# A hybrid decoder layer on one core: the low-rank products of decay and rate from stacked rounded parts

## The chip, the core and the metric

The kernel runs on one core of one Trainium2 chip. TensorE multiplies and transposes, VectorE (DVE in the profile), ScalarE (ACT) and GpSimd (POOL) do the element work, SyncE (SP) issues most of the DMAs, and each engine takes its own program in order, with semaphores between them. The metric is the device time of one launch, in microseconds. Before the change it is 3192.13 us, the median of three runs (3189.84 to 3195.04).

## The reference

One layer on a prompt of 2048 rows and, beside it, 8 sequences of 4 sample rows with stored state. A row has 1024 columns. The normalised rows go through one wide projection into a short gated convolution and an RWKV-7 recurrence of 16 heads of 64 columns. The two are merged by gates and projected back. Cut to the part around the change:

```python
h = _rmsnorm(x, norm_g)
p = jnp.einsum('bsd,dn->bsn', h, w_in)          # 10368 columns
...
xm = p_rwkv + (prev - p_rwkv) * mu_shift
r, k, v, wd, ad, zr = _split(xm, RWKV_SIZES)    # wd and ad: 64 columns each
w_logit = w0 + jnp.einsum('bsr,rc->bsc', jnp.tanh(wd), w_up)
w_log = (-jax.nn.softplus(-w_logit.astype(jnp.float32)) - 0.5)
decay = jnp.exp(-jnp.exp(w_log))
a = jax.nn.sigmoid((a0 + jnp.einsum('bsr,rc->bsc', ad, a_up)).astype(jnp.float32))
...
S = (S * d_t[:, :, None, :] + sa[..., None] * (kk_t * a_t)[:, :, None, :]
     + v_t[..., None] * k_t[:, :, None, :])
y = jnp.einsum('bhvk,bhk->bhv', S, r_t)
```

The two low-rank products are the `einsum` with `w_up` (the decay, from `tanh(wd)`) and the one with `a_up` (the rate, from `ad`). Each contracts over 64 columns and gives 1024.

## The kernel before

**Sets, pairs, blocks.** The prompt rows are taken in four sets (`th` 0 to 3) of `NT` = 512, transposed so that columns lie on the partitions; the last set has the 32 sample rows beside its 512 and the stored rows behind them. Per set the projection runs through blocks of 128 weight columns (`Block`). A block's weights (1024 x 128) are two rounded parts, `whl`: the high part is a copy into the F32R type, the low part what remains. In the first set both are made from `wraw` (ACT copies, DVE subtracts, L236 and L249) and stored in scratch; later sets load them back. `proj` (L266) issues 24 matmuls per block and 512 columns: for each eighth of the contraction high weights by high rows `XH`, low weights by `XH`, and high weights by `XL`, all into the bank `ip`. They are the bulk of TensorE's program. Weights are fetched up to `WAHEAD` = 4 blocks ahead.

**Side programs.** A set has 8 pairs of heads, 128 columns each, so 32 pairs in all. A pair's work beyond the projection stands in generators, each a `Side` (L309): `rwkv_keys` (norms, low-rank products, decay, scaled keys `AR` and `BK`), `rwkv_solve` (scores `GM` and the inversion of triangular blocks: `Mc`, its transposed form `Mi`, and 31 steps of `tt` and `X`), `rwkv_merge` (from `Xo` to the inverse `Xbd`, with the small products through `T11` and `Wm`), `rwkv_load` (`SV`, `BKt`), `rwkv_chain` (the state) and `rwkv_out`. `drive` (L351) walks the projection matmul by matmul and after each lets the sides go on; how far, a planner decides: each side has a weight (`SIDES`, L25) to be spent over a stretch of the main stream (`over`, `CUTS`), and goes on only when `Clock`, a model of the engines' times fed by each traced instruction (L111 to L153), says that its operands will be ready and its banks free. So what one instruction is thought to cost decides where later ones of all sides stand. The order on each engine is then fixed in the program. All instructions go through one helper, so the profile gives them L121; they are told apart by their tiles.

**The state chain.** `rwkv_chain` (L1091) takes a pair's eight chunks of 64 rows, each a step: `pa` (state `S` by `AR`), `us` (two DVE additions), `pb` from `us` and `Xbd`, `SV` (one half copied by DVE, then one by ACT), `pb` from `SV` and `BKt`, and the update of `S` (two on DVE, with `sp` from ACT). Each waits for the one ahead of it; on TensorE projections are laid between them. While pair k is in its chain, keys, solve, merge and load of pair k + 1 run on the same engines.

**The low-rank products.** `lora_block` (L763) is the set's first block of the recurrence: its 128 output columns are `wd` and `ad`. `alloc` forces the keys of the set before to their end (`need`), since those read the one tile `lora`; `end` takes the tanh of the upper 64 partitions. In `rwkv_keys` (L808) SP loads the pair's 64 x 128 of `w_up` and of `a_up` into the two halves of `up`; two plain fp32 matmuls, each over 64 partitions, fill two banks `pt`, and ACT takes a tanh of each (with the biases `w0h` and `a0h`). A +1 on ACT and a scan on DVE, with the mask `rst`, follow. An fp32 matmul shows as two passes in the trace, an F32R one as one.

Of the kernel before, what the change touches and what calls it, by code (L numbers as in the profile page):

```python
# [7 lines left out]
F32 = mybir.dt.float32  # L8
# [171 lines left out]
def hybrid_kernel(tc, x_prompt, x_sample, state_conv, state_shift, state_rwkv, norm_g, w_in, conv_w,  # L180
# [238 lines left out]
    SV = xp.tile([P, NC1, P], F32, name="SV")  # L419
    early = {}  # L420
# [69 lines left out]
    rst = con.tile([P, NT], F32, name="rst")  # L490
    V.memset(rst, 1.0)
    V.memset(rst.rearrange("p (c t) -> p c t", t=C)[:, :, 0:1], 0.0)
    rst_s = con.tile([P, NSAMP], F32, name="rst_s")
# [265 lines left out]

    cur = {}  # L760
    job = {}

    def lora_block(th):  # L763

        def alloc():
            need(job.get(("keys", th * NB - 1)))
            return rw.tile([P, NT + NSAMP], F32, name="lora")

        def end(t):
            nt = NTT[th]  # L770
            A.activation(out=t[0:64, 0:nt], in_=t[0:64, 0:nt], func=AF.Tanh)
            cur["lora"] = t
        return mixed_block(th, ("lora", th), WCOL[:, RW0 + 3 * D:RW0 + 3 * D + P], 3 * NB, alloc, end)

# [28 lines left out]
    HS = [slice(0, 64), slice(64, 128)]  # L803

# [3 lines left out]
    def rwkv_keys(th, p, o):  # L808
# [7 lines left out]
        up = sm.tile([P, P], F32, name="up")  # L816
        for k, src in enumerate((w_up, a_up)):
            SP.dma_start(out=up[HS[k]], in_=src[0][:, p * P:(p + 1) * P])

# [14 lines left out]
        yield W["norm"], [up], 2  # L834
# [4 lines left out]
        for (c0, c1) in sg:  # L839
            if c0:  # L840
                yield 0.0, (), 2
            pts = [new_pt([P, 512], F32, name="pt") for _ in range(2)]
            for k in range(2):
                T.matmul(pts[k][:, 0:c1 - c0], lhsT=up[HS[k]], rhs=lt[HS[k], c0:c1], start=True, stop=True)
            for k, (dst, bias) in enumerate(((L, w0h), (ta, a0h))):
                A.activation(out=dst[:, c0:c1], in_=pts[k][:, 0:c1 - c0], func=AF.Tanh, scale=0.5, bias=bias[:, p:p + 1])
# [134 lines left out]
    def rwkv_merge(th, p, o):  # L981
# [8 lines left out]
        T11 = rw.tile([P, NCH, 32], F32, name="T11")  # L990
# [3 lines left out]
        Wm = rw.tile([P, NCH, 32], F32, name="Wm")  # L994
# [404 lines left out]
    for t in (BK[:, NCH], ARB[0][:, NCH], ARB[1][:, NCH], *XB):  # L1399
        G.memset(t, 0.0)  # L1400
# [11 lines left out]
    def begin_pair(th, p, total):  # L1412
# [7 lines left out]
        job["keys", k] = Side(rwkv_keys(th, p, o), "keys", [prior("load", k - 1), prior("solve", k - 1)] + read(k - 2)).over(0, f[3])  # L1420
# [20 lines left out]
    for th, hv, p, nx in plan:  # L1441
        total = length(hv)
        if p is None:
            job["prep", 0, 1] = Side(prep(0, 1), "first").over(0, EDGE / 2 * NB)
            Side(zero_rest(), "zero").over(1.5 * NB, 2 * NB)
# [177 lines left out]
```

## Time and profile before

| | |
|---|---|
| time, median of 3 runs | 3192.13 us |
| the profiled execution | 3193.32 us, of which the span (first to last instruction) is 3191.6 |
| granted TensorE clock, mean | 0.992 |
| projections `ip<-XH,whl` and `ip<-XL,whl` | 7776 and 3888 matmuls, 2105.1 and 1364.0 us busy |
| low-rank products `pt<-lora,up` | 160 passes, 46.8 us busy |
| first matmul group of the low-rank products, last one | 63.0 us, 2506.6 us |
| TensorE busy from 25 to 760 us | 705.90 of 735 |
| TensorE busy from 760 to 1395 us | 624.22 of 635 |
| TensorE busy from 2900 us to the end | 278.30 of 291.6 |

Matmuls overlap their neighbours, so busy sums of groups exceed what the groups cost; the cost of a few matmuls is read from the starts of those around them. In rows of the time line the columns are the start, the duration, the engine, the line, the operation, output<-inputs, for matmuls the tile of the array, the shape, and how many like instructions in succession the row stands for; in brackets stands how long the engine had idled and for what. In rows of equal stretches the busy times of PE, PEld, DVE, ACT and POOL follow the length, then granted clock, DMA share and GB/s.

### The profile page before, as it was taken

The numbers are of one execution on the slowest core, as the hardware profiler recorded it, in microseconds if no ns is written. First come the engines' busy times: TensorE is split into PE (matmuls) and PEld (weight loads), VectorE is DVE, ScalarE is ACT, GpSimd is POOL, SyncE is SP. The second block draws the span as 40 slices with busy tenths as digits, with TensorE's granted clock in tenths as the row PEclk, the third lists the DMA queues.
The fourth block names the chain that finished last, engine by engine and source line by source line (L and its number), as shares of the span: only waits on it lengthen the run. The fifth ranks groups of instructions, "written<-read, shape, count | busy, mean of one in ns | idle before, by whom it ended". The sixth has DMA issues, their size and how long they took to land.

```text
span 3191.6 us, 55625 instructions
## 1 busy us (share of the span) xinstructions
PE 3092.0 (97%) x21530; PEld 2596.5 (81%) x21530; DVE 1992.5 (62%) x5704; ACT 1241.9 (39%) x2571; POOL 309.6 (10%) x517
## 2 busy tenths in 40 slices
PE   7999999999999999999999999999999999999998
PEld 6777777887777778877777789989889889778896
DVE  5687777776666666666666676766677664443332
ACT  5454445444333434434443334344444432211201
POOL 2011111111000001100101010000000000000000
PEclk9999999999999999999999999999999999999999
DMA  8786666644444444444444444434443469988863
GB/s 267 258 267 220 213 212 220 207 173 148 146 162 160 155 159 159 169 157 153 159 153 158 159 147 142 138 127 139 144 143 135 138 223 318 363 337 304 316 241 120
DMA packets 241504, 615.09 MB, mean 193 GB/s; under 512 B 33931, under 2 KB 143620, under 8 KB 187479
## 3 DMA queue, kind: packets, MB, share of 16 engines
q1 hardware_dynamic: 241094, 611.00, 55.8%
q8 instruction: 170, 2.79, 0.4%
q14 instruction: 96, 0.78, 0.1%
q0 software_dynamic: 144, 0.52, 0.0%
HBM read 452.10 MB, written 159.36 MB: 192 GB/s over the span
## 4 chain that ended last, share of the span: by engine, by line
PE 69%; DVE 18%; ACT 5%; issue 5%; DMA 3%; POOL 1%; SPq 0%; ACTq 0%; DVEq 0%; POOLq 0%
PE ip L121 49%; PE pt L121 10%; PE po L121 6%; PE pb L121 3%; DVE X L121 2%; DVE tmp L121 2%; DVE tt L121 2%; ACT tmp L121 2%; DVE Mi L121 2%; DVE whl L121 1%; DVE us L121 1%; PE pa L121 1%; DVE S L121 1%; DMA wraw<-in_w_in_dram 1%; ACT Xbd L121 1%
## 5 line engine op out<-in xcount | busy, mean ns | idle before, releaser
L121 PE MATMUL ip<-XH,whl 128*128 128x512 f32 (+3 forms) x7776 | 2105.1, 351 | 6.6 <-DVE gt L121 3.9
L121 PEld LDWEIGHTS ip<-XH,whl 128*128 128x128 f32 x7776 | 1342.0, 190 | 178.3 <-issue 27.5
L121 PE MATMUL ip<-XL,whl 128*128 128x512 f32 (+3 forms) x3888 | 1364.0, 351 | 2.7 <-POOL XL L121 2.6
L121 PEld LDWEIGHTS ip<-XL,whl 128*128 128x128 f32 x3888 | 738.5, 190 | 79.0 <-issue 7.0
L121 DVE TENSOR_TENSOR X<-X,tt 128x60 f32<-128x60 f32 (+24 forms) x992 | 211.7, 213 | 27.5
L121 DVE TENSOR_TENSOR tt<-Mi,X 128x60 f32<-128x60 f32 (+24 forms) x992 | 209.9, 212 | 27.4
L121 DVE SCALAR_TENSOR_TENSOR S<-pb,pe,sp 64x64 f32<-64x64 f32 x512 | 143.8, 281 | 106.6 <-PE pb L121 100.5
L121 ACT ACTIVATE sp<-S,pe 128x128 f32<-128x128 f32 x256 | 99.5, 400 | 244.7 <-DVE S L121 241.2
L121 ACT ACTIVATE tmp<-ip,vec 128x512 f32<-128x512 f32 (+2 forms) x174 | 103.2, 593 | 231.6 <-PE ip L121 230.2
L121 ACT COPY SV<-pb 64x64 f32<-64x64 f32 x256 | 53.3, 208 | 329.2 <-DVE SV L121 325.5
L121 DVE TENSOR_TENSOR whl<-wraw,whl 128x1024 fp32r<-128x1024 f32 x105 | 134.2, 1279 | 58.0 <-ACT whl L121 57.7
L121 PE MATMUL po<-whl,MH 128*128 128x512 f32 x544 | 170.4, 394 | 0.0
L121 DVE TENSOR_TENSOR us<-pa,P 64x64 f32<-64x64 f32 x512 | 110.2, 215 | 45.2 <-PE pa L121 33.7
L121 PEld LDWEIGHTS pb<-us,Xbd 128*128 128x128 f32 x512 | 85.9, 189 | 56.9 <-PE ip L121 21.5
L121 PE MATMUL ip<-RH,whl 128*128 128x512 f32 (+2 forms) x512 | 128.4, 341 | 1.7 <-DMA whl<-w_or 1.6
L121 PEld LDWEIGHTS pb<-SV,BKt 128*128 128x128 f32 x512 | 85.1, 189 | 54.6 <-ACT SV L121 45.9
L121 ACT CAST whl<-wraw 128x1024 fp32r<-128x1024 f32 x105 | 109.5, 1044 | 50.5 <-DMA wraw<-in_w_out_r_dram 14.8
L121 PE MATMUL pb<-SV,BKt 128*128 128x128 f32 x512 | 107.3, 291 | 17.4 <-ACT SV L121 17.3
L121 DVE TENSOR_TENSOR GM<-pt,mask_p 128x512 f32<-128x512 f32 x128 | 82.4, 685 | 64.4 <-PE pt L121 64.4
L121 PEld LDWEIGHTS po<-whl,MH 128*128 128x128 f32 x544 | 102.2, 188 | 24.0 <-DVE whl L121 0.3
L121 PE MATMUL pb<-us,Xbd 128*128 128x64 f32 x512 | 90.1, 258 | 23.7 <-DVE us L121 23.1
L121 ACT COPY Xbd<-Xo 32x256 f32<-32x256 f32 x128 | 88.1, 688 | 64.0 <-DVE Xo L121 61.9
(494 smaller groups left out, 3838.6 us busy)
## 6 DMA issues: line engine op xcount, KB each, us to landing
wraw<-in_w_in_dram SPq DMA_DIRECT2D x81, 512.0 KB
whl<-w_k SPq DMA_DIRECT2D x24, 1024.0 KB
whl<-w_r SPq DMA_DIRECT2D x24, 1024.0 KB
whl<-w_v SPq DMA_DIRECT2D x24, 1024.0 KB
whl<-w_z SPq DMA_DIRECT2D x24, 1024.0 KB
whl<-w_xin SPq DMA_DIRECT2D x24, 1024.0 KB
whl<-w_cg SPq DMA_DIRECT2D x24, 1024.0 KB
whl<-w_zc SPq DMA_DIRECT2D x24, 1024.0 KB
```

The source lines that it names most:

```text
L121: r = f(*a, **k)
```

## The change

The rows `tanh(wd)` and `ad` are split once per set, in `end` of the block, into two F32R tiles: `lora0` for the decay has the rounded high part in its upper 64 partitions and the remainder in the lower 64, `lora1` for the rate has them the other way round. The block's own result is now a tile of the pool `tmp`, and the forced end of the last keys stands in `end`. A new side, `up_parts`, runs once in the first set: it loads `w_up` and `a_up`, each twice, one below the other, rounds them (ACT, all 128 partitions), makes the low parts (DVE, 64 partitions) and stores both in the scratch `up_d`. Per pair four loads fetch its 128 columns of these into the one tile `UP`, whose low parts have the other 64 partitions set to zero at the start. The products are four F32R matmuls over 128 partitions in place of two fp32 ones over 64: high weights by the stacked rows, then low weights by the same rows, added up in the bank; for the 32 sample rows likewise. The masks `rst` and `rst_s` become BF16, and two tiles of the merge (`T11`, `Wm`) now take the buffers of `Mc` and `X`.

```diff
--- before.py
+++ after.py
@@ -417,6 +417,9 @@
     GMB = [xp.tile([P, NC1, 2, 2, C], F32, name=f"GM{i}") for i in range(2)]
     XB = [xp.tile([P, NC1, P], F32, name=f"Xbd{i}") for i in range(2)]
     SV = xp.tile([P, NC1, P], F32, name="SV")
+
+    UP = xp.tile([P, 4, P], F32R, name="UP")
+    up_d = [[dram.tile([P, 2, 4 * P], F32, name=f"up{k}_{q}") for q in range(NB // 4)] for k in range(2)]
     early = {}
 
     def load_early(i):
@@ -487,10 +490,10 @@
                         base=0, channel_multiplier=1)
     V.transpose(X0.rearrange("p a b -> p (a b)"), xo0.rearrange("p a b c -> p (a b c)"))
 
-    rst = con.tile([P, NT], F32, name="rst")
+    rst = con.tile([P, NT], BF16, name="rst")
     V.memset(rst, 1.0)
     V.memset(rst.rearrange("p (c t) -> p c t", t=C)[:, :, 0:1], 0.0)
-    rst_s = con.tile([P, NSAMP], F32, name="rst_s")
+    rst_s = con.tile([P, NSAMP], BF16, name="rst_s")
     V.memset(rst_s, 1.0)
     V.memset(rst_s.rearrange("p (c t) -> p c t", t=SL)[:, :, 0:1], 0.0)
 
@@ -757,20 +760,42 @@
                 Block(("bg", th, b), wcol(D, b), bg_evac, None, bg_end),
                 gate("gc", GT0, gc_d), gate("gr", GT0 + D, gr_d)]
 
+    HS = [slice(0, 64), slice(64, 128)]
     cur = {}
     job = {}
 
     def lora_block(th):
 
         def alloc():
+            return tmp.tile([P, TW], F32, name="tmp")
+
+        def end(t):
             need(job.get(("keys", th * NB - 1)))
-            return rw.tile([P, NT + NSAMP], F32, name="lora")
-
-        def end(t):
             nt = NTT[th]
             A.activation(out=t[0:64, 0:nt], in_=t[0:64, 0:nt], func=AF.Tanh)
-            cur["lora"] = t
+            parts = []
+            for k in range(2):
+                L = rw.tile([P, NT + NSAMP], F32R, name=f"lora{k}")
+                A.copy(L[HS[k], 0:nt], t[HS[k], 0:nt])
+                V.tensor_tensor(out=L[HS[1 - k], 0:nt], in0=t[HS[k], 0:nt], in1=L[HS[k], 0:nt].bitcast(F32), op=ALU.subtract)
+                parts.append(L)
+            cur["lora"] = parts
         return mixed_block(th, ("lora", th), WCOL[:, RW0 + 3 * D:RW0 + 3 * D + P], 3 * NB, alloc, end)
+
+    def up_parts():
+
+        for k, src in enumerate((w_up, a_up)):
+            for q in range(NB // 4):
+                raw = tmp.tile([P, TW], F32, name="tmp")[:, 0:4 * P]
+                for h in range(2):
+                    SP.dma_start(out=raw[HS[h]], in_=src[0][:, 4 * q * P:4 * (q + 1) * P])
+                yield 1, [raw]
+                h, l = (tmp.tile([P, TW], F32R, name="tmp")[:, 0:4 * P] for _ in range(2))
+                A.copy(h, raw)
+                V.tensor_tensor(out=l[HS[k]], in0=raw[HS[k]], in1=h[HS[k]].bitcast(F32), op=ALU.subtract)
+                yield 1, [h, l[HS[k]]]
+                SP.dma_start(out=up_d[k][q][:, 0], in_=h.bitcast(F32))
+                SP.dma_start(out=up_d[k][q][HS[k], 1], in_=l[HS[k]].bitcast(F32))
 
     def rkvz_blocks(th, p):
         nt = NTT[th]
@@ -800,8 +825,6 @@
                 mixed_block(th, ("z", th, p), wcol(RW0 + 3 * D + P, p), 3 * NB + 1 + p,
                             lambda: tmp.tile([P, TW], F32, name="tmp"), z_end)]
 
-    HS = [slice(0, 64), slice(64, 128)]
-
     def cview(t):
         return t[:, 0:NT].rearrange("p (c t) -> p c t", t=C)
 
@@ -813,9 +836,10 @@
         n, nt = NT, NTT[th]
         sg = [(0, n)] + ([(n, nt)] if samp else [])
 
-        up = sm.tile([P, P], F32, name="up")
-        for k, src in enumerate((w_up, a_up)):
-            SP.dma_start(out=up[HS[k]], in_=src[0][:, p * P:(p + 1) * P])
+        for k in range(2):
+            c = slice(p % 4 * P, (p % 4 + 1) * P)
+            SP.dma_start(out=UP[:, 2 * k].bitcast(F32), in_=up_d[k][p // 4][:, 0, c])
+            SP.dma_start(out=UP[HS[k], 2 * k + 1].bitcast(F32), in_=up_d[k][p // 4][HS[k], 1, c])
 
         sq = tmp.tile([P, TW], F32, name="tmp")
         A.activation(out=sq[:, 0:nt], in_=kT[:, 0:nt], func=AF.Square, scale=vc("kk", p))
@@ -831,7 +855,7 @@
             T.matmul(pt[0:NSAMP, 0:2], lhsT=sq[:, n:nt], rhs=bone2, start=True, stop=True)
             V.tensor_scalar(out=ss[0:NSAMP, 2 * TPS:], in0=pt[0:NSAMP, 0:2], scalar1=1e-24, scalar2=None, op0=ALU.max)
             V.reciprocal(ss[0:NSAMP, 2 * TPS:], ss[0:NSAMP, 2 * TPS:])
-        yield W["norm"], [up], 2
+        yield W["norm"], [UP], 2
 
 
         L = tmp.tile([P, TW], F32, name="tmp")
@@ -841,7 +865,8 @@
                 yield 0.0, (), 2
             pts = [new_pt([P, 512], F32, name="pt") for _ in range(2)]
             for k in range(2):
-                T.matmul(pts[k][:, 0:c1 - c0], lhsT=up[HS[k]], rhs=lt[HS[k], c0:c1], start=True, stop=True)
+                for i in range(2):
+                    T.matmul(pts[k][:, 0:c1 - c0], lhsT=UP[:, 2 * k + i], rhs=lt[k][:, c0:c1], start=i == 0, stop=i == 1)
             for k, (dst, bias) in enumerate(((L, w0h), (ta, a0h))):
                 A.activation(out=dst[:, c0:c1], in_=pts[k][:, 0:c1 - c0], func=AF.Tanh, scale=0.5, bias=bias[:, p:p + 1])
         yield W["lora"]
@@ -987,11 +1012,11 @@
             A.copy(Xbd[g, 0:NCH, g].rearrange("p c (a e) -> p c a e", e=4),
                                                  Xo[g].rearrange("p a e c -> p c a e"))
 
-        T11 = rw.tile([P, NCH, 32], F32, name="T11")
+        T11 = rw.tile([P, NCH, 32], F32, name="Mc")
         for h in range(2):
             V.transpose(T11[blk[2 * h]], Xbd[blk[2 * h], 0:NCH, blk[2 * h]])
         yield W["bt"], [T11[0:96], Mo[64:96]], 1
-        Wm = rw.tile([P, NCH, 32], F32, name="Wm")
+        Wm = rw.tile([P, 8, 32], F32, name="X")
         pt = new_pt([P, 512], F32, name="pt")
         for c in range(NCH):
             for h in range(2):
@@ -1396,7 +1421,7 @@
     ncv = xp.tile([P, NB, 2 + 2 * NS], F32, name="ncv")
     xsmp = xp.tile([P, NB, R], F32, name="xsmp")
     scv = xp.tile([P, NB, 2 * NS], F32, name="scv")
-    for t in (BK[:, NCH], ARB[0][:, NCH], ARB[1][:, NCH], *XB):
+    for t in (UP[64:128, 1].bitcast(F32), UP[0:64, 3].bitcast(F32), BK[:, NCH], ARB[0][:, NCH], ARB[1][:, NCH], *XB):
         G.memset(t, 0.0)
 
     def zero_rest():
@@ -1417,7 +1442,7 @@
         f = [total * x for x in CUTS["end" if end_(th, p) else "most" if th < LAST else "last"]]
         def read(n):
             return [prior(x, n) for x in ("chain", "samp")]
-        job["keys", k] = Side(rwkv_keys(th, p, o), "keys", [prior("load", k - 1), prior("solve", k - 1)] + read(k - 2)).over(0, f[3])
+        job["keys", k] = Side(rwkv_keys(th, p, o), "keys", [prior("load", k - 1), prior("solve", k - 1), prior("up", 0)] + read(k - 2)).over(0, f[3])
         job["solve", k] = Side(rwkv_solve(th, p, o), "solve", [job["keys", k], prior("merge", k - 1)] + read(k - 2)).over(f[3], f[4])
         job["merge", k] = Side(rwkv_merge(th, p, o), "merge", [job["solve", k]] + read(k - 2)).over(f[4], f[5])
         job["load", k] = Side(rwkv_load(th, p, o), "load", [job["keys", k]] + read(k - 1)).over(f[4], f[5])
@@ -1442,6 +1467,7 @@
         total = length(hv)
         if p is None:
             job["prep", 0, 1] = Side(prep(0, 1), "first").over(0, EDGE / 2 * NB)
+            job["up", 0] = Side(up_parts(), "first").over(1.5 * NB, 4 * NB)
             Side(zero_rest(), "zero").over(1.5 * NB, 2 * NB)
         else:
             if before:
```

With the new matmuls the planner's clock runs otherwise, and the order on each engine changes in many places. Three of them in one steady pair, the third set's second chain, follow.

First TensorE at the low-rank product of the next pair, before, beside a chain step: `ip` are projections, `pb<-SV,BKt` ends a step of the chain, and `pa` begins the next one.

```order
L121 MATMUL ip<-XL,whl 128x512
L121 MATMUL pt<-lora,up 128x512 x2
L121 MATMUL ip<-XH,whl 128x512
L121 MATMUL pb<-SV,BKt 128x128
L121 MATMUL ip<-XH,whl 128x512
L121 MATMUL ip<-XL,whl 128x512
L121 MATMUL ip<-XH,whl 128x512 x2
L121 MATMUL ip<-XL,whl 128x512
L121 MATMUL ip<-XH,whl 128x512 x2
L121 MATMUL pa<-S_472,AR_203 128x128
```

The same place after the change.

```order
L121 MATMUL ip<-XL,whl 128x512
L121 MATMUL ip<-XH,whl 128x512
L121 MATMUL pb<-SV,BKt 128x128
L121 MATMUL pt<-lora_13408,UP 128x512 x2
L121 MATMUL pt<-lora_13411,UP 128x512 x2
L121 MATMUL ip<-XH,whl 128x512
L121 MATMUL ip<-XL,whl 128x512
L121 MATMUL ip<-XH,whl 128x512 x2
L121 MATMUL ip<-XL,whl 128x512
L121 MATMUL ip<-XH,whl 128x512 x2
L121 MATMUL pa<-S_477,AR_203 128x128
```

The products stood ahead of `pb<-SV,BKt`, as two groups of two passes, and stand behind it now, as four 128-row matmuls; seven projections stand behind them before `pa`, as before.

On ACT, which reads the products, at the same place of the next pair, before (`sp` is the scaled state, the first `tmp<-tmp` the +1 ahead of the scan).

```order
L121 COPY SV<-pb 64x64
L121 ACTIVATE tmp<-pt,w0h 128x512
L121 ACTIVATE tmp<-tmp 128x512
L121 ACTIVATE tmp<-pt,a0h 128x512
L121 ACTIVATE sp<-S_473,pe 128x128
```

And after.

```order
L121 COPY SV<-pb 64x64
L121 ACTIVATE tmp<-pt,w0h 128x512
L121 ACTIVATE tmp<-pt,a0h 128x512
L121 ACTIVATE tmp<-tmp 128x512
L121 COPY tmp<-ip 128x512
L121 ACTIVATE sp<-S_478,pe 128x128
```

Both tanh now stand ahead of the +1, and an evacuation of the projection ahead of `sp`.

Second, VectorE around `Mi`, from the end of the fourth step on, before (`us<-pa`, `SV` and `S` belong to the chain of one pair, `GM`, `Mc` and `Mi` to the solve of the next, `bv` and the first `tmp<-tmp` to its keys).

```order
L121 TENSOR_TENSOR tmp<-tmp 128x512
L121 COPY SV<-pb 64x64
L121 SCALAR_TENSOR_TENSOR S_472<-pb,pe,sp 64x64 x2
L121 TENSOR_TENSOR bv<-pt,vT 128x512
L121 TENSOR_TENSOR us<-pa,P_15062 64x64 x2
L121 TENSOR_TENSOR GM_206<-pt,mask_p 128x8x64 x2
L121 COPY SV<-pb 64x64
L121 TENSOR_TENSOR GM_206<-pt,mask_p 128x8x64 x2
L121 SCALAR_TENSOR_TENSOR S_472<-pb,pe,sp 64x64 x2
L121 TENSOR_TENSOR cv<-ip,cv 128x512
L121 TENSOR_TENSOR us<-pa,P_15062 64x64 x2
L121 STREAM_TRANSPOSE Mi<-Mc 128x1024
```

And after.

```order
L121 TENSOR_TENSOR tmp<-tmp 128x512
L121 TENSOR_TENSOR us<-pa,P_15177 64x64 x2
L121 COPY SV<-pb 64x64
L121 TENSOR_TENSOR bv<-pt,vT 128x512
L121 SCALAR_TENSOR_TENSOR S_477<-pb,pe,sp 64x64 x2
L121 TENSOR_TENSOR GM_206<-pt,mask_p 128x8x64 x2
L121 TENSOR_TENSOR us<-pa,P_15177 64x64 x2
L121 TENSOR_TENSOR cv<-ip,cv 128x512
L121 TENSOR_TENSOR GM_206<-pt,mask_p 128x8x64 x2
L121 COPY SV<-pb 64x64
L121 STREAM_TRANSPOSE Mi<-Mc 128x1024
L121 SCALAR_TENSOR_TENSOR S_477<-pb,pe,sp 64x64 x2
```

`GM` stood on either side of `SV`, behind `us`, and `Mi` stood behind the fifth update of `S` and the sixth `us`; now `Mi` stands between `SV` and the update of `S` of the fifth step, and the subtraction `tmp<-tmp` ahead of a `us`.

Third, VectorE at the end of the inversion, where the merge begins, before (`Yc` and `mu` are the output of the pair ahead, `T` is `T11`).

```order
L121 SCALAR_TENSOR_TENSOR kT<-ip,omu,tmp 128x512
L121 TENSOR_TENSOR Yc<-pt,Yc 128x512
L121 STREAM_TRANSPOSE Xo<-X 128x256
L121 TENSOR_REDUCE mu__15591<-Yc 128x8
L121 STREAM_TRANSPOSE T_15653<-Xbd_208 32x256
L121 TENSOR_SCALAR mu__15591<-mu__15591 128x8
L121 TENSOR_TENSOR Yc<-Yc,mu__15591 128x512
L121 STREAM_TRANSPOSE T_15653<-Xbd_208 32x256
L121 TENSOR_REDUCE mu__15591<-tmp 128x8
```

And after, where `T11` reads as `Mc`.

```order
L121 TENSOR_TENSOR tt<-Mi,X 128x16
L121 TENSOR_REDUCE mu__15709<-Yc 128x8
L121 TENSOR_TENSOR X<-X,tt 128x8x2
L121 TENSOR_SCALAR mu__15709<-mu__15709 128x8
L121 TENSOR_TENSOR tt<-Mi,X 128x8
L121 TENSOR_TENSOR Yc<-Yc,mu__15709 128x512
L121 TENSOR_TENSOR X<-X,tt 128x8
L121 STREAM_TRANSPOSE Xo<-X 128x256
L121 TENSOR_REDUCE mu__15709<-tmp 128x8
L121 STREAM_TRANSPOSE Mc<-Xbd_208 32x256
```

ACT at the same place, before and then after (`X<-pt` is `Wm` in its new buffer).

```order
L121 COPY SV<-pt 64x4x128 x2
L121 COPY Xbd_208<-Xo 32x8x32 x4
L121 COPY X<-X_248 128x256
L121 ACTIVATE tmp<-Yc 128x512
L121 COPY BKt<-pt 128x512
L121 ACTIVATE tmp<-ip,vec 128x512
L121 COPY Wm<-pt 32x256 x2
```

```order
L121 COPY SV<-pt 64x4x128 x2
L121 ACTIVATE tmp<-Yc 128x512
L121 COPY Xbd_208<-Xo 32x8x32 x4
L121 COPY BKt<-pt 128x512
L121 ACTIVATE tmp<-ip,vec 128x512
L121 COPY X<-pt 32x256 x2
```

`Xo` now stands behind the mean of `Yc` and its subtraction, and the square of `Yc` on ACT ahead of the copies to `Xbd`; the copy of the constant to `X` has left this place.

## The prediction

> **What bounds the kernel now.** I read the page first, then stretches of equal length, then single instructions on the time line. All times are in us.
>
> ```profile
> span 3191.6 us, 55625 instructions
> PE 3092.0 (97%) x21530; PEld 2596.5 (81%) x21530; DVE 1992.5 (62%) x5704; ACT 1241.9 (39%) x2571; POOL 309.6 (10%) x517
> ...
> PE 69%; DVE 18%; ACT 5%; issue 5%; DMA 3%; POOL 1%; SPq 0%; ACTq 0%; DVEq 0%; POOLq 0%
> ```
>
> TensorE is busy 97% and holds 69% of the chain of waits. VectorE holds 18% of it: TensorE takes its program in order, and where an instruction of the state chain stands in it before its operand is ready, all projections behind it wait too. So two things count: what the matmuls cost, and where the chain stands in each engine's order.
>
> ```profile
> 846.74:921.54 74.80, 73.87 (x484) 57.91 (x483) 47.70 (x146) 30.02 (x63) 7.45 (x14) 1.00 0.45 155
> ...
> 382.00:460.00 78.00, 75.25 (x483) 58.70 (x483) 58.86 (x156) 39.45 (x73) 9.72 (x15) 1.00 0.68 217
> ```
>
> These are one pair of the second set and one of the first (length, then PE, PEld, DVE, ACT, POOL busy, granted clock, DMA share, GB/s). The old order is the same in most pairs of sets 2 and 3, so one worked-out pair stands for many.
>
> **The products themselves.**
>
> ```profile
> 849.15 0.39 PE L121 MATMUL ip<-XL,whl 128*128 128x512 f32 x1
> 849.47 1.13 PE L121 MATMUL pt<-lora,up 64*128 64x512 f32 x4
> 850.53 0.50 PE L121 MATMUL ip<-XH,whl 128*128 128x512 f32 x1
> 850.87 0.38 PE L121 MATMUL pb<-SV,BKt 128*128 128x128 f32 x2
> ...
> 1481.96 0.63 PE L121 MATMUL pt<-tmp,bones 128*128 128x512 f32 x2
> 1482.42 0.40 PE L121 MATMUL ip<-XH,whl 128*128 128x512 f32 x1
> ```
>
> Two products of rounded parts with bones, 128 rows and 512 columns like the new ones, move the program on by 1482.42 - 1481.96 = 0.46: 0.235 each, as a projection does. Old: from 849.15 to 850.87 is 1.72; less two projections (0.47) the old products cost 1.25, with the change into 64-row tiles and back. New: four, 4 x 0.235 = 0.94, and no change of tiles. Gain 0.31 a pair, 32 x 0.31 = 9.8.
>
> ```profile
> 2008.70 0.28 PE L121 MATMUL ip<-XH,whl 128*128 128x256 f32 x1
> 2008.91 0.57 PE L121 MATMUL pt<-lora,up 64*128 64x32 f32 x4
> 2009.42 0.38 PE L121 MATMUL ip<-XH,whl 128*128 128x256 f32 x1
> 2009.64 0.38 PE L121 MATMUL pb<-SV,BKt 128*128 128x128 f32 x2
> ...
> 2037.12 0.75 PE L121 MATMUL pt<-tmp,bones 128*128 128x512 f32 x4
> 2037.73 0.38 PE L121 MATMUL ip<-XH,whl 128*128 128x288 f32 x1
> ```
>
> The 32 sample rows of a pair cost 2009.64 - 2008.70 = 0.94 less two projections of 0.12: 0.70. Two wide and two 32-wide products with bones took 0.61 together, so a 32-wide one (0.61 - 0.46) / 2 = 0.07, four 0.3: gain 0.4 x 8 pairs = 3.4. Together **-13.2**.
>
> The Trainium skill speaks against this edit: TensorE: Matmul & The Clock Gate, Why this matters for your kernels, advises that products over fewer than 128 rows be put on separate row groups, where they run side by side, since a small one alone takes as long as a full one. The trace agrees that the old ones ran side by side (four passes in 1.13); what the rule leaves open is the price of a pass, and bones gives it.
>
> ```profile
> 304.45 2.04 PE L121 MATMUL pt<-lora,up 64*128 64x512 f32 x4
> ...
> 305.37 0.29 PEld L121 LDWEIGHTS pt<-lora,up 64*128 64x128 f32 x2 [0.62 <-DVE ss L121]
> ```
>
> In four pairs of the first set they did not: the weights of the second product waited 0.62 for VectorE to read the norms out of the bank, and the block took 2.04 in place of 1.13. This wait belongs to the bank, not to the products. In the new order of VectorE the norms (ss) stand behind two more instructions of the output there, so I count it as kept (0); if it goes, -0.9 x 4.
>
> **What else is added.** Per set two copies and two subtractions of 64x512, some 0.6 and 0.7 each: four blocks of 24 projections (5.6 each) stand between them and their reader, so 0. The forced end of the last pair's keys moves by one block, also ahead of these: 0. Per pair SP issues four loads for two, into one buffer whose readers are a pair earlier: 0. The masks in BF16: no row shows a scan of mixed types; I take 0, between -0.2 and +0.2 a pair. At the start SP issues eight loads (1.0 MB) and eight stores (1.6 MB), and ACT and DVE do four splits.
>
> ```profile
> 25.00:45.00 20.00, 17.17 (x126) 16.84 (x127) 10.12 (x16) 7.94 (x12) 3.19 (x6) 0.84 0.79 247
> 45.00:65.00 20.00, 20.00 (x96) 15.80 (x95) 7.80 (x10) 7.67 (x13) 0.67 (x4) 1.00 0.95 325
> ```
>
> ACT (7.94 of 20) and DVE (10.12) have room. The DMA engines are 79 to 95% busy, and 2.6 MB at the 247 to 325 GB/s moved there are 9 us of their time. Weights are fetched up to three blocks (17 us) ahead, which hides most: **+2**, bounds 0 and +9.
>
> **What the moved order costs in a steady pair.** I set the old durations into the new order. Time 0 is the fifth state product (pa), as in the second excerpt of the order.
>
> ```profile
> 1486.34 1.16 PE L121 MATMUL pt<-AR,BK 64*128 64x128 f32 x16
> ...
> 1487.54 1.29 DVE L121 TENSOR_TENSOR GM<-pt,mask_p 128x512 f32<-128x512 f32 x2 [1.50 <-PE pt L121]
> ...
> 1490.05 0.45 DVE L121 TENSOR_TENSOR us<-pa,P 64x64 f32<-64x64 f32 x2
> 1490.53 2.07 DVE L121 STREAM_TRANSPOSE Mi<-Mc 128x1024 f32<-128x1024 f32 x1
> ...
> 1488.26 1.65 ACT L121 COPY Mc<-GM 32x256 f32<-32x256 f32 x4 [1.98 <-DVE GM L121]
> ...
> 492.31 2.04 DVE L121 STREAM_TRANSPOSE Mi<-Mc 128x1024 f32<-128x1024 f32 x1 [0.61 <-ACT Mc L121]
> ...
> 494.97 0.41 PE L121 MATMUL pb<-us,Xbd 128*128 128x64 f32 x2 [1.12 <-DVE us L121]
> ```
>
> Mi needs four copies Mc (0.41 each), these need the masked scores GM. Before, the update of S and the next us stood ahead of Mi; now S stands behind it. The second half of the scores stands four projections behind pa and starts at 1.25; GM starts 1.2 later and lasts 1.29, to 3.74. ACT makes three copies to 4.4 (the first two need only half of GM), then its half of SV to 4.6, and pb<-SV starts at 4.7. The fourth copy ends at 5.06, Mi at 7.15, S at 7.63, and the next pa can start at 7.7. Between pb<-SV and pa stand eight projections, 2.0 with pb<-SV itself: TensorE is there at 6.7. Wait **+1.0**. The first set shows that such a wait is real: there us stands behind Mi, and PE idles 1.12. In the next two steps three projections stand where six stood; the operations between cost 0.7 there, about as much as the old order lost at these places, so 0.
>
> ```profile
> 1479.22 1.52 DVE L121 TENSOR_TENSOR tmp<-tmp 128x512 fp32r<-128x512 f32 x1
> ...
> 1481.17 0.49 PE L121 MATMUL pb<-SV,BKt 128*128 128x128 f32 x2 [0.67 <-ACT SV L121]
> ```
>
> This subtraction stood between us and SV and cost 0.67. Now it stands ahead of us; its input is ready 0.3 after pa, with 1.2 to 1.5 of its own us ends 0.45 too late: **-0.2**.
>
> ```profile
> 1462.54 0.69 ACT L121 ACTIVATE tmp<-pt,w0h 128x512 f32<-128x512 f32 x1 [1.87 <-PE pt L121]
> ...
> 1463.99 1.23 DVE L121 TENSOR_TENSOR_SCAN tmp<-rst,tmp 128x512 f32<-128x512 f32 x1 [0.28 <-ACT tmp L121]
> ```
>
> The scan stands ahead of the second step's us. The products now stand behind pb<-SV, not ahead of it, and ACT does both tanh (0.7 each) before the +1 (0.6) that the scan reads. From pb<-SV: first tanh at 0.95, scan at 2.9, its end 4.1, us 4.6, pb<-us 4.7, where TensorE is at 4.5: **+0.2**.
>
> ```profile
> 1511.58 0.43 DVE L121 STREAM_TRANSPOSE Xo<-X 128x256 f32<-128x256 f32 x1
> ...
> 1513.29 0.69 DVE L121 TENSOR_TENSOR Yc<-Yc,mu__15591 128x512 f32<-128x512 f32 x1
> 1514.19 0.43 DVE L121 STREAM_TRANSPOSE T<-Xbd 32x256 f32<-32x256 f32 x1 [0.21 <-ACT Xbd L121]
> ...
> 1512.04 2.81 ACT L121 COPY Xbd<-Xo 32x256 f32<-32x256 f32 x4 [1.11 <-DVE Xo L121]
> 1515.18 0.63 ACT L121 ACTIVATE tmp<-Yc 128x512 f32<-128x512 f32 x1
> ...
> 1517.81 0.74 ACT L121 COPY Wm<-pt 32x256 f32<-32x256 f32 x2 [0.80 <-PE pt L121]
> ...
> 1517.07 0.21 PE L121 MATMUL pt<-T,GM 32*32 32x32 f32 x1
> ...
> 1518.74 0.69 PE L121 MATMUL pt<-Xbd,Wm 32*32 32x32 f32 x32
> ```
>
> Third excerpt: the last steps of the inversion and Xo now stand behind the mean of the output, and the square ahead of the copies to Xbd. On the old clock Xo then ends at 1514.55, the square at 1514.65, the four copies at 1517.45 (were 1514.85), the second T at 1517.35; TensorE asks at 1517.07, and with the hand-over it is 0.4 late. Then ACT still has BKt (0.6) and an evacuation (0.6) ahead of the two Wm copies (0.74): they end at 1519.5, where TensorE would be at 1519.1, another 0.45. **+0.85**.
>
> Sum of a steady pair 1.0 - 0.2 + 0.2 + 0.85 = 1.85; bounds 0.3 (the two large ones mostly hidden) and 2.5. The new order repeats this word for word in 9 windows and nearly in two more: 10.5 x 1.85 = **+19** (3 to 26). In the first set's four like pairs the same count finds the wait at Mi as before (1.2), about 2 less ahead of the first two steps, and 2.5 more at the eighth, where a weight block's low part now stands ahead of us: +0.5 a pair, **+2** (-6 to +6). In the last set, us is done 0.9 after pa starts (0.42 until it starts, 0.45 long) and pb<-us can follow at 1.0; at 16 steps less than that stands between the two, at 9 before. Seven more at 0.25: **+2** (-4 to +6).
>
> **Sum:** -13.2 + 2 + 19 + 2 + 2 = +12 on the profiled execution's 3193.3: 3205. That execution is 1.2 above the median 3192.1; for the median I forecast **3204**.
>
> **Rivals.**
> - *Covered waits (faster).* Place: S behind Mi, and Xbd behind the square. The projections between pb<-SV and pa cover Mi if it starts 1.0 earlier than I count; the copies to Xbd are covered if they start 0.85 earlier. For it: in the old steady pair Mi waited for nothing. Against it: four copies of 0.41 bind Mi to GM. Then a steady pair costs 0, and -13 + 2 = -11 gives 3181. Chance 0.17.
> - *One of the two covered.* A steady pair costs 0.9: 10.5 x 0.9 = 9, and -13 + 9 + 4 = 0 gives 3192. Chance 0.25.
> - *First weights late.* All 9 us of the start's transfers show in place of 2: 3211. Chance 0.08.
> - *The products are not cheaper.* If a new one took what a pass of an old one takes (1.06 / 2 = 0.53 from start to start), four cost 2.1, 0.87 more than before: +28 with +25 of the rest, 3245. Against it: bones, 0.235. Chance 0.02. The section on small products in the Trainium skill's TensorE: Matmul & The Clock Gate warns of this direction.
>
> **How the numbers follow.** Forecast 0.48. Faster by over 0.2% (6.4 us, about what a measurement of this kernel can tell from no change): 0.17; within: 0.25; slower: 0.48 + 0.08 + 0.02 = 0.58. The range goes from the covered case to the forecast with the upper bound of the steady pairs (3204 + 7) and part of the start's: 3180 to 3216.
>
> **What would show it.** The new products at 0.235 spacing with no change of tiles; a steady pair of 74.80 - 0.31 + 1.85 = 76.3; once a pair, a pa that waits some 1.0 for DVE S; the Wm product waiting for ACT; no new wait for weights before 100. If steady pairs come back at 74.5, the price of the order was wrong and the time is near 3181; if they do not and the time is still low, the first or the last set has gained what I could only bound.

## The result, and the profile after

The changed kernel takes **3211.01 us** (median of 6 runs, 3207.64 to 3217.57) against 3192.27 for the kernel before on the same chips: a ratio of 1.0064, 95% interval 1.0048 to 1.0080. Forecast were 3204, with a range of 3180 to 3216. The sign and the size were about right, by luck as the last sections show. The place was not: the profile and the runs below put the loss at the start of the first set, where the forecast had 2 us, and none of it in the steady pairs, where it had 19.

The page of the changed kernel (busy time and share of the span by engine):

```profile
span 3207.7 us, 55770 instructions
PE 3088.6 (96%) x21530; PEld 2619.6 (82%) x21530; DVE 1978.9 (62%) x5716; ACT 1249.0 (39%) x2583; POOL 311.2 (10%) x519
```

16.1 more of span with 3.4 less of TensorE's work: TensorE waits more. Where, two stretches show that answer to those of before, one pair of the second set and one of the first (length, then PE, PEld, DVE, ACT, POOL busy, granted clock, DMA share, GB/s):

```profile
861.20:935.80 74.60, 73.59 (x484) 58.41 (x483) 46.64 (x147) 29.89 (x63) 7.51 (x14) 1.00 0.46 158
403.30:483.60 80.30, 76.99 (x483) 62.25 (x483) 57.26 (x156) 39.65 (x74) 10.50 (x15) 0.96 0.66 210
```

The steady pair takes 74.60 where it took 74.80; 76.3 was forecast. A pair of the first set takes 80.30 where one took 78.00. So I set the starts of the same projections (11664 in both, in the same sequence) beside each other, after minus before:

| projection | start before, us | after minus before, us |
|---|---|---|
| 338 | 94.2 | -0.7 |
| 370 | 105.5 | +10.5 |
| 506 | 146.4 | +19.5 |
| 1000 | 312.4 | +8.6 |
| 2000 | 627.1 | +12.5 |
| 3000 | 917.4 | +15.2 |
| 6000 | 1815.1 | +14.0 |
| 10440 | 2653.7 | +9.8 |
| 11000, and all behind it | 2735.3 | +16.5 |

These are one execution of each kernel, and a single point moves by some microseconds because other work now stands elsewhere between the same projections; what lasts is a loss between 95 and 150 us of which 9 to 15 remain, next to nothing over sets 2 and 3, a gain of 4 in the last set, and a loss of 7 in the last pair and behind it.

### The profile page after: what moved, and what is told of

Same layout as the page of the kernel before. It is cut to its first block, busy times and chain, and to the rows that moved or that the text cites. A ratio compares the mean times of both kernels' runs of the same rounds, so it can differ in the third digit from the quotient of the medians.

```text
span 3207.7 us, 55770 instructions
## 1 busy us (share of the span) xinstructions
PE 3088.6 (96%) x21530; PEld 2619.6 (82%) x21530; DVE 1978.9 (62%) x5716; ACT 1249.0 (39%) x2583; POOL 311.2 (10%) x519
## 5 line engine op out<-in xcount | busy, mean ns | idle before, releaser
L121 PEld LDWEIGHTS pa<-S,AR 128*128 128x128 f32 x512 | 86.9, 189 | 38.2 <-DVE S L121 26.5
L121 PE MATMUL pa<-S,AR 128*128 128x128 f32 x512 | 102.5, 282 | 11.8 <-DVE S L121 11.6
```

What stands on the lines that cost most here:

```text
L121: r = f(*a, **k)
```

## What happens at the start

Six stretches of the kernel before, then five of the changed one, in the columns of above:

```profile
95.00:102.00 7.00, 7.00 (x50) 5.77 (x50) 3.14 (x5) 2.16 (x5) 0.00 (x0) 1.00 1.03 366
102.00:109.00 7.00, 7.00 (x36) 5.71 (x35) 5.77 (x14) 6.74 (x12) 0.30 (x2) 1.00 1.05 397
109.00:116.00 7.00, 7.00 (x34) 5.70 (x33) 6.34 (x24) 3.71 (x6) 0.73 (x1) 1.00 0.98 296
116.00:130.00 14.00, 11.88 (x80) 9.19 (x78) 10.53 (x38) 5.31 (x9) 0.45 (x2) 1.00 0.63 187
130.00:137.00 7.00, 6.16 (x14) 4.65 (x15) 3.17 (x7) 5.06 (x9) 2.42 (x1) 0.53 0.70 277
...
151.00:165.00 14.00, 14.00 (x113) 10.28 (x113) 7.25 (x19) 7.26 (x14) 0.19 (x1) 0.76 0.64 197
```

```profile
95.00:102.00 7.00, 4.04 (x19) 3.12 (x17) 1.58 (x3) 3.78 (x9) 0.61 (x1) 1.00 0.95 349
102.00:109.00 7.00, 4.83 (x16) 3.33 (x17) 5.78 (x9) 4.46 (x8) 0.49 (x3) 0.56 0.94 308
109.00:116.00 7.00, 7.00 (x34) 5.45 (x33) 4.23 (x7) 1.17 (x3) 0.00 (x0) 0.71 1.01 369
...
137.00:145.00 8.00, 0.49 (x3) 0.05 (x1) 4.84 (x23) 5.91 (x10) 2.48 (x2) 0.71 0.35 90
145.00:151.00 6.00, 5.98 (x18) 4.49 (x19) 2.68 (x3) 1.85 (x2) 0.00 (x0) 0.53 0.60 208
```

In the changed kernel TensorE idles twice, and each time the clock is granted at 0.53 to 0.71 for a while behind it. The kernel before has two stretches of low clock too (0.53 and 0.76), later and with little or no waiting. Single instructions of the changed kernel on the time line (idle time ahead, and what ended it, in brackets), TensorE first, then ACT:

```profile
102.12 0.66 PE L121 MATMUL pt<-ident,tmp 128*128 128x128 f32 x4 [3.08 <-ACT tmp L121]
...
105.62 0.79 PE L121 MATMUL pt<-tmp,bones 128*128 128x512 f32 x1 [1.75 <-ACT tmp L121]
...
145.01 0.79 PE L121 MATMUL ip<-XH,whl 128*128 128x512 f32 x1 [7.52 <-ACT whl L121]
...
99.23 1.06 ACT L121 ACTIVATE tmp<-wraw 128x1024 bf16<-128x1024 f32 x1 [3.22 <-DMA wraw<-in_x_prompt_dram]
...
101.46 0.60 ACT L121 COPY tmp<-ss 128x512 f32<-128x512 f32 x1
...
126.94 1.04 ACT L121 CAST whl<-wraw 128x1024 fp32r<-128x1024 f32 x1
...
140.63 2.65 ACT L121 COPY Xbd<-Xo 32x256 f32<-32x256 f32 x4 [1.42 <-DVE Xo L121]
...
143.93 2.92 ACT L121 CAST whl<-wraw 128x1024 fp32r<-128x1024 f32 x3
```

First place: ACT takes its program in order and waits 3.22 for a later row of the prompt (its statistics belong to `late_setup`, L589, whose rows share the four buffers `wraw` with the raw weights). Behind it stands the copy of the norms that the first pair's keys hand to TensorE (101.46), and TensorE idles 3.08, then 1.75. Up to 106 us the waits are 5.1 in all, 0.29 of them for weights. The clock then costs some 4.83 x 0.44 + 7.00 x 0.29 = 4.2 more, over the time that TensorE was busy there: 9.3 of the 11.2 between the first two rows of the table. The Trainium skill, TensorE: Matmul & The Clock Gate, HAM oscillation, warns of idle gaps above some 3.4 us. Here the longest was 3.08, in a stretch of 7 with 4.04 of work. In the kernel before the clock fell behind waits of 1.02 at most (130 to 137) and once with TensorE counted as busy throughout (151 to 165), so the length of a gap does not settle it; what does was not tried.

Second place: from 126.94 to 143.93 ACT rounds no weights. The next three casts stand behind the copies to `Xbd` of the first pair, which wait for its inversion on VectorE; TensorE uses up the block that it is in and the one whose weights are ready, some 5.6 each, and idles 7.52, with a low clock behind it. Before, the casts stood behind these copies too, but the copies began at 126.04 and not at 140.63: the casts came at 129.07, 131.00 and 134.13, and the waits from 95 to 160 were 3.0 in all.

Between 150 and 159 us of the old time line some 7 of the loss come back (from +21.0 to +14.1). There the kernel before has its low clock of 151 to 165 and some 5 us of other products between two projections.

## The experiments

The rivals for the start were A, SyncE's queue (stores of parts that wait there for their splits, weights behind them); B, the bytes; C, the order that the planner makes of being told of `up_parts`. In all fences below `...` stands for lines left out.

**The queue.** The DMAs of `up_parts` issued by GpSimd:

```diff
+    def dma_start(self, out, in_, eng=None):
+        r = (eng or self.eng).dma_start(out=out, in_=in_)
...
+  SP.dma_start(out=up_d[k][q][:, 0], in_=h.bitcast(F32), eng=nc.gpsimd)
```

> The changed kernel with one edit: the loads and stores of up_parts are issued by GpSimd in place of SyncE; all else, the splits and the bytes moved, stays. Of the 18.7 us by which the changed kernel is slower, 15.8 arise between the 290th and the 520th projection, where TensorE waits for weights. Theory A (SyncE's queue: each store of parts waits there for its split, and the loads of weights stand behind it): the loss in that stretch falls to 0 to 5 and the time to 3196 to 3200. Theory B (the 2.6 MB more that the DMA engines move): nothing changes, 3208 to 3214. Theory C (another order of ACT and VectorE in the first pair, through the planner): 3208 to 3214 as well.

Measured: 3213.43, ratio 1.0065 (1.0053 to 1.0077). This is what B and C expected and A did not, but it decides nothing by itself, since SyncE now waited for the stores in front of the first loads of `UP` (idle time of its queue):

```profile
SPq L172 <- DMA up<-tmp: 11.6, 2, 10.6
```

So again, with the first pair's four loads of `UP` on GpSimd's queue too:

> The changed kernel with the loads and stores of up_parts on GpSimd's queue, as before, and with the first pair's four loads of UP there too: in the first trial these stood in SyncE's queue and waited 10.6 us for the stores on the other one, so that trial did not free the queue. Theory A (SyncE's queue): 3195 to 3201. Theories B (bytes) and C (the planner's order of the first pair): 3208 to 3215.

Measured: 3209.50, ratio 1.0055 (1.0043 to 1.0068). With nothing of the parts in SyncE's queue until the second pair the time stays: A is not the cause of the whole. At the start it has a share. In the profiled executions the 370th projection, where the changed kernel is 10.5 behind, is 4.0 and 3.8 behind in these two runs, so the first place is smaller by more than half without these DMAs in SyncE's queue. The second place is there in both (TensorE waits 7.0 and 5.6 for ACT's `whl`), and at 247 us they are 9.5 and 5.3 behind, the changed kernel 11.2. The second run then loses 9 in the last pair and behind it.

**Constant weights.**

```diff
-  SP.dma_start(out=UP[:, 2 * k].bitcast(F32), in_=up_d[k][p // 4][:, 0, c])
-  SP.dma_start(out=UP[HS[k], 2 * k + 1].bitcast(F32), in_=up_d[k][p // 4][HS[k], 1, c])
...
+    for j in range(4):
+        G.tensor_copy(UP[:, j], ident)
```

> The changed kernel without up_parts and without any load of UP: its four parts are filled once, by GpSimd, with the identity matrix, so the low-rank products take constant weights and the output is not the reference's. The planner is told of the splits as before. Theories A and B (SyncE's queue, bytes): the loss of 15.8 at the start is gone, 3194 to 3197. Theory C (order): most of it stays, 3205 to 3211. The steady pair stays at 74.6 in all of them.

Measured: 3188.59, ratio 0.9990 (0.9981 to 0.9998). That is 22.4 below the changed kernel and below what any of the three expected. Taken alone it speaks for A and B, since the loss at the start is gone. But the planner is told of the splits only and of no DMA here, so the order is another one too, and the run does not part the three.

**The parts alone.** The kernel before with `up_parts` added:

```diff
+            job["up", 0] = Side(up_parts(), "first").over(1.5 * NB, 4 * NB)
```

> The kernel before, with up_parts alone added (its parts are made and stored, and nothing reads them); the low-rank products stay the old ones. Theories A and B: the start loses what it lost in the changed kernel, 3192 + 12 to 16 = 3204 to 3208. Theory C (order that comes from the new products): 3191 to 3195.

Measured: 3215.22, ratio 1.0075 (1.0063 to 1.0087): 23 us without a single new product, more than any of the three expected. The loss does not come of an order made for the new products. Against A and B this says nothing yet, since the planner is told and reorders the first pair here too.

**The products alone, in almost the old order.**

```diff
+  for i in range(2):
+      T.eng.matmul(pts[k][:, 0:c1 - c0], lhsT=bones, rhs=lt[:, c0:c1], start=i == 0, stop=i == 1)
+  clock.add("PE", [pts[k][:, 0:c1 - c0]], [up[HS[k]], lt[HS[k], c0:c1]], 0.84 * 2 * max(P, c1 - c0) / 1.9 + ..., 200.0)
```

> The kernel before, with the two fp32 products of a pair replaced by four F32R products over 128 rows, of bones and the whole lora tile (rounded when written), so the values are not the reference's; the planner is told the cost of the old ones, and the order on every engine stays the old one almost row for row. This is the direct gain without the moved order. By the prediction's term (0.31 a pair and 0.4 more with sample rows): 3192.2 - 13.2 = 3179, and a steady pair of 74.80 - 0.31 = 74.49. If the moved order is what holds the steady pair at 74.61, its price is 0.12 a pair and not 1.85. Rival (the old products cost no more than the new ones where they stand): 3190 to 3194 and 74.8.

Measured: 3178.46, ratio 0.9952 (0.9940 to 0.9964): -13.8, where -13.2 was worked out. A steady pair of this run:

```profile
841.11:915.77 74.66, 73.56 (x485) 58.40 (x484) 47.72 (x147) 30.05 (x63) 7.44 (x14) 1.00 0.45 154
```

74.66, so the direct gain is only 0.15 there; half of the 0.31 goes into waits of the chain (those for `SV` and `us` are 1.6 longer over thirteen pairs). The rest comes from the first set (4 us by 627, half a microsecond a pair) and from what stands behind 1815 us (6 us). And the changed kernel's 74.60 is no longer than this: **in a steady pair the moved order costs nothing.**

**Bytes alone, order alone.** In the kernel before, first the eight loads and eight stores on GpSimd's queue, unknown to the planner, so that TensorE, VectorE, ScalarE and SyncE keep the old order:

```diff
+  nc.gpsimd.dma_start(out=raw[HS[h]], in_=src[0][:, 4 * q * P:4 * (q + 1) * P])
...
+  nc.gpsimd.dma_start(out=up_d[k][q][:, 0], in_=raw)
+  nc.gpsimd.dma_start(out=up_d[k][q][HS[k], 1], in_=raw[HS[k]])
```

> The kernel before, with the eight loads and eight stores of up_parts (2.6 MB, unsplit and read by nobody) issued by GpSimd and not told to the planner: the order of TensorE, VectorE, ScalarE and SyncE stays that of before. Theory B (bytes): 3204 to 3215. Theories A and C: 3190 to 3195.

Measured: 3191.45, ratio 1.0001 (0.9992 to 1.0010). Then the reverse: the planner is told of every DMA and split, and nothing is issued.

```diff
+  def dma_start(self, out, in_, ghost=False):
+      r = None if ghost else self.eng.dma_start(out=out, in_=in_)
...
+  clock.add("ACT", [h], [raw], 200 + 0.84 * 512)
+  clock.add("DVE", [l[HS[k]]], [raw[HS[k]], h[HS[k]]], 150 + 1.05 * 512)
```

> The kernel before, where the planner is told of all that up_parts does (its DMAs on SyncE and its splits) and nothing of it is issued: the order becomes that of the run with the parts alone (3215), with no byte more. Theory C (the order): 3207 to 3216. Theories A and B: 3190 to 3195, since neither a store that waits nor a byte is added.

Measured: 3206.33, just under what C expected, ratio 1.0048 (1.0035 to 1.0060): **+15 us from an order alone**, with not a byte and not an instruction more. Its time line, TensorE and then ACT, shows the second place of above again:

```profile
137.81 0.79 PE L121 MATMUL ip<-XH,whl 128*128 128x512 f32 x1 [7.37 <-ACT whl L121]
141.65 0.79 PE L121 MATMUL ip<-XH,whl 128*128 128x512 f32 x1 [3.05 <-DVE whl L121]
...
119.67 1.04 ACT L121 CAST whl<-wraw 128x1024 fp32r<-128x1024 f32 x1
...
133.01 2.64 ACT L121 COPY Xbd<-Xo 32x256 f32<-32x256 f32 x4 [2.11 <-DVE Xo L121]
...
136.73 1.03 ACT L121 CAST whl<-wraw 128x1024 fp32r<-128x1024 f32 x1
```

So C holds for about two thirds of the 23. The other 9 (3215.2 - 3206.3) are what the DMAs and splits cost once they stand in nearly that order; the single runs lie close (3210.9 to 3223.7 against 3202.0 to 3213.0), so the 9 is rough. In the old order, off SyncE, the bytes cost 0. What the splits alone cost there was not run. Nor is the first place one of order alone: at the 370th projection this run is 3.7 behind, the run with the parts 11.4. By the 520th the two are 21.9 and 25.7 behind, so half of that difference is lost again in the second place.

**Telling the planner nothing.** The changed kernel, with `up_parts` by the engines directly and GpSimd's queue:

> The changed kernel with up_parts issued without telling the planner (its DMAs and the first pair's four loads of UP on GpSimd's queue, the same bytes, the same splits): the loads of weights and of later rows in SyncE's first hundred instructions then alternate almost as in the kernel before. Theory C (what costs is the order that the planner makes of being told): the start's loss of 15 goes, 3211 - 15 to 20 = 3191 to 3196. If the splits or the stores that wait cost too, wherever they stand: 3197 to 3204.

Measured: 3212.74, ratio 1.0065 (1.0051 to 1.0078), a miss of the expected 3191 to 3196. From 94 to 150 us this run loses 9 (+11.4 and +20.3 against the kernel before) where the changed kernel loses 22, but it has lost 11 at 71:

```profile
71.39 1.87 PE L121 MATMUL pt<-bone,tmp 128*128 128x2 f32 x8 [8.52 <-ACT tmp L121]
```

```profile
ACT tmp L794 <- DMA tmp<-in_a_up_dram: 14.6, 2, 8.0
```

The first line is TensorE's time line, the second ACT's idle time (sum, times, longest; L794 is the split of parts in that kernel's numbering). ACT stands at a split whose raw rows have not come. It is the same fault at another load: an ACT instruction that waits for a DMA holds what TensorE needs next.

**Taking the later rows away from the start.** `late_setup` begun with the third pair:

```diff
-            if (th, p) == (0, 0):
+            if (th, p) == (0, 2):
                 Side(late_setup(), "late").over(0, 0.9 * total)
```

> The changed kernel with late_setup (the statistics of the later rows, whose twelve loads take the four buffers of the raw weights) begun with the third pair in place of the first. If the loss comes of rows that stand ahead of weights in these four buffers while the first pair runs: 3193 to 3199, and no wait for weights from 100 to 150. If it comes of the moved chain and keys of the first pair (their steps stand 30 us earlier): 3206 to 3212.

> The control: the kernel before with the same move of late_setup alone. If the rows were harmless there: 3190 to 3195. If they cost the kernel before something as well (its four waits for weights up to 150): 3183 to 3189.

Measured: 3202.10 (ratio 1.0033, 1.0020 to 1.0046) with the change, 3211.28 (1.0057, 1.0044 to 1.0069) without it, neither as expected. By the 800th projection (246.8 us in the kernel before) the two are 11.1 and 10.4 us ahead of the kernel before, the changed kernel 11.2 behind: without these rows beside it, making the parts costs nothing at the start. By the 1200th the block of rows, now in the third pair, has cost 14 and 17 (24 without the change by 627 us). So these rows cost the kernel before some 10 us too where they stand, and more as a block in the third pair.

**Spreading them.** One row at a time, over five and a half pairs:

```diff
+        for i in range(TPS, NTL + 1):
+            xt, m = load_x(i)
+            yield 0.2, [xt]
+            stat_tile(i, xt, m)
+            yield 0.8
...
-                Side(late_setup(), "late").over(0, 0.9 * total)
+                Side(late_setup(), "late").over(0.2 * total, 5.5 * total)
```

> The changed kernel with the twelve later rows and the sample rows loaded one at a time, each just ahead of its statistics, and spread over five and a half pairs of the first set in place of one. If the change loses its 15 us because rows and parts together stand ahead of weights at the start: no wait for weights up to 150 and no block of rows in a later pair either, 3183 to 3193, below the changed kernel by 18 or more and below the kernel before. If the parts cost whatever stands beside them: 3199 to 3208.

> The kernel before with the same spreading alone. Moved as a block to the third pair the rows gave 10 us at the start and cost 24 in that pair. Spread out: 3180 to 3188. The difference between the two runs of this call is what the change is worth once the start is relieved: -13.8 (direct gain, as measured in the old order) and some 4 to 10 of the moved order in the last set, -10 to -3, if the parts are then free; +5 or more if they are not.

Measured, with the change: 3187.42, 23.6 below the changed kernel, and the same as the kernel before within the measurement (ratio 0.9994, 0.9985 to 1.0003). Without the change: 3194.40 (1.0007, 0.9998 to 1.0016), not the expected 3180 to 3188: it is 10 ahead at 376 us as hoped, and gives that back by the end of the first set. TensorE's waits from 20 to 160 us in the spread changed kernel (sum, times, longest):

```profile
PE ip L121 <- DVE BKt L121: 4.8, 1, 4.8
PE ip L121 <- POOL XL L121: 0.6, 1, 0.6
PE pt L121 <- ACT X L121: 0.2, 1, 0.2
```

Both waits of the changed kernel are gone, and with the rows spread in both kernels the change is worth 3187.4 - 3194.4 = -7 (the means of the eleven runs differ by 4.8). The planner makes a new order here as well, so the rows and the order around them go together in this run.

## Why the forecast came out near, point by point

**The products, -13.2: the total right** (-13.8), in part by luck, since it is spread otherwise than worked out: 0.15 and not 0.31 in a steady pair, more in the first set, where the wait of the weights for the norms, counted as kept, goes in part (in those four pairs 1.97 from the first product to the next projection became 1.58, elsewhere 1.06 became 0.93). In the changed kernel the row of the new products:

```profile
865.04 0.38 PE L121 MATMUL pb<-SV,BKt 128*128 128x128 f32 x2
865.18 1.17 PE L121 MATMUL pt<-lora,UP 128*128 128x512 f32 x4
866.19 0.39 PE L121 MATMUL ip<-XH,whl 128*128 128x512 f32 x1
```

Four products in 866.19 - 865.18 = 1.01, against 0.94 from bones.

**The start, +2 with bounds 0 and +9: this step failed.** It read "ACT and DVE have room", weighed the bytes and let the weights' lead hide them. The bytes cost 0, and the start lost 14.5 (table below). Room on an engine over 20 us says nothing of an in-order program in which one instruction waits for a load. The order excerpts were taken from the steady pair only; the first pair's order, which the planner made anew because `up_parts` stands on its clock, was not read. The rival "first weights late" had the place and, by chance, the time (3211), but not the mechanism: it summed 9 us of transfers.

**The steady pair, +1.85: failed by cancelling.** The largest term was followed nearly to the instruction. The changed kernel, TensorE, VectorE and ACT at the fifth step:

```profile
1499.80 0.38 PE L121 MATMUL pa<-S,AR 128*128 128x128 f32 x2
...
1502.24 1.29 DVE L121 TENSOR_TENSOR GM<-pt,mask_p 128x512 f32<-128x512 f32 x2 [0.31 <-PE pt L121]
...
1504.47 0.40 ACT L121 COPY Mc<-GM 32x256 f32<-32x256 f32 x1
...
1504.91 2.07 DVE L121 STREAM_TRANSPOSE Mi<-Mc 128x1024 f32<-128x1024 f32 x1 [1.25 <-ACT Mc L121]
1506.91 0.56 DVE L121 SCALAR_TENSOR_TENSOR S<-pb,pe,sp 64x64 f32<-64x64 f32 x2
...
1507.52 0.49 PE L121 MATMUL pa<-S,AR 128*128 128x128 f32 x2 [0.69 <-DVE S L121]
```

From `pa` at 0, `Mi` ends at 1506.98 - 1499.80 = 7.18 (7.15 was forecast), `S` at 7.67 (7.63), the next `pa` starts at 7.72 (7.7). TensorE got there at 7.0 and not 6.7, so the wait is 0.69 for 1.0. The other terms are what failed. The subtraction ahead of `us` took 0.69 in the new place and not the 1.52 of the old row:

```profile
1493.87 0.69 DVE L121 TENSOR_TENSOR tmp<-tmp 128x512 fp32r<-128x512 f32 x1
...
1494.04 1.67 POOL L121 TENSOR_TENSOR cv<-cv,tmp 128x512 f32<-128x512 f32 x1 [12.37 <-DVE tmp L121]
```

so the old wait of 0.67 goes whole, not by 0.2. The +0.2 ahead of the second step does not show either: the waits for `us` below become fewer and shorter in sum. And the merge's 0.85 does not appear: `Mi`, and with it the inversion, runs 0.6 earlier against TensorE's program than on the old clock, from which I had taken the inversion's end without the advance of my own first term. The second `T11` is done at 1531.32, and TensorE's products with it start at 1532.07 without waiting. TensorE's waits over thirteen steady pairs, before and then after (sum, times, longest), show the exchange:

```profile
PE pb L121 <- ACT SV L121: 9.6, 15, 0.9
PE pb L121 <- DVE us L121: 3.3, 12, 0.3
...
PE pa L121 <- DVE S L121: 0.3, 1, 0.3
```

```profile
PE pa L121 <- DVE S L121: 7.8, 12, 0.7
PE pb L121 <- ACT SV L121: 1.7, 3, 0.9
PE pb L121 <- DVE us L121: 1.5, 2, 0.9
```

0.6 a pair for `S` is new, 0.75 for `SV` and `us` is gone. This is read from traces, and the old-order run (74.66) confirms that the order's terms sum to nothing; they were not tried one by one.

**The sum.** The old-order run has the direct gain without order and parts, so the changed kernel minus that run, at the same projections of the two profiled executions (one of each, so good to a few microseconds), gives both by stage:

| stage (time in the kernel before) | forecast, us | measured, us |
|---|---|---|
| start, to 247 us | +2 | +14.5 |
| rest of the first set and two pairs of the second, to 857 | +2 | +6.0 |
| the rest of sets 2 and 3, to 1815 | +19 | +0.8 |
| last set, to 2654 | +2 | +1.5 |
| last pair and output | 0 | +6.9 |
| direct gain, whole | -13.2 | -13.3 |
| sum | +12 | +16.4 |

The forecast came near because errors met: 12.5 too little at the start, 4 in the rest of the first set (within its bounds of -6 to +6) and 7 at the end, against 18 too much in steady pairs. For the end the forecast had no term at all. Of the 7 there 2.8 are one wait of the first output projections for `gt` on VectorE, 6.7 against 3.9 before; with the rows spread it stands at 6.7 as well. Where the other 4 come from was not tried.

## What to carry to other kernels

Where a planner sets the order, a small piece of set-up work costs what the planner does with it: compare the order around that work first, and there above all on each in-order engine the instructions that wait for a load or for another engine, and what TensorE needs from behind them. A "hidden" load needs a buffer, a place in a queue and a place on the engine that reads it, and bandwidth is only a fourth condition. When a new order is worked out by hand, carry each advance forward as well as each delay, and don't take over the duration of a row that ran beside another engine's work.

## What the runs showed of the hardware

Behind waits of 3.08, 0.29 and 1.75 us on TensorE the granted clock stood at 0.56 and 0.71 for 14 us; 5.1 us of waiting were followed by some 4 us of slower work. In the kernel before it stood at 0.53 from 130 to 137 us behind waits of 1.02 at most, and at 0.76 from 151 to 165 us with TensorE counted as busy all the time.

A subtraction of 128x512 on VectorE, the one into the rounded `tmp`, took 1.52 where GpSimd's product (1.28) ran beside it from the start, and 0.69 where VectorE was there first and GpSimd took 1.67: whichever came second paid. It is so for all the rows of this kind. In the kernel before 14 of 24 subtractions came second and took 1.52 to 1.73; in the changed one 12 of 24 came first, took 0.68 or 0.69, and the product beside them 1.66 to 1.67; those with no product beside them took 0.68 to 0.70 in both.

And 2.6 MB more through GpSimd's queue raised the share of the DMA engines from 0.79 to 0.96 (25 to 45 us) and from 0.95 to 0.99 (45 to 65 us), and changed the time by nothing that can be measured (1.0001, 0.9992 to 1.0010).
